# Gates of the first 1024 tokens by seven quarter products, and attention's row sums with three direct products per group

## The chip, the cores and the metric

The kernel runs on one core of a Trainium2 chip. The time is device time in microseconds (us) from the start to the end of one execution. The engines are named as the profile names them: PE does matrix products (PEld its weight loads), DVE, ACT and POOL do elementwise work, SP issues most of the DMAs; SPq, POOLq and ACTq are the DMA queues that SP, POOL and ACT feed.

## The reference, cut to what matters

One layer over 2048 latent tokens of width 1024, with 256 context tokens. Both parts that are changed stand in these lines:

```python
mod_l = (s_lat @ w_mod[l] + b_mod[l])[:, None, :]
sh1, sc1, g1, sh2, sc2, g2 = jnp.split(mod_l, 6, axis=-1)
h = _modulate(_rms(x, norm1_g[l]), sh1, sc1)
p = h @ w_in[l]                                   # 1024 -> q, kv, k_pe, f, gates
...
s = jnp.einsum('bqhd,bkhd->bhqk', q, k) * (QK_DIM ** -0.5)
pr = jax.nn.softmax(s, axis=-1)                   # 2048 queries, 2304 keys, 8 heads
o = jnp.einsum('bhqk,bkhd->bqhd', pr, v)
...
ga = jax.nn.sigmoid(p[..., OFF_GA:OFF_GB])        # 1024 columns
gb = jax.nn.sigmoid(p[..., OFF_GB:N_IN])          # 1024 columns
x = x + g1 * ((ga * (attn_o @ w_o_attn) + gb * (four_o @ w_fourier)) @ w_out)
```

A mixture of experts follows on the result; the change does not touch it.

## The kernel before, in words

**Number format.** PE multiplies in fp32r. For close to fp32 accuracy each factor is kept as a high part (a cast, ACT) and a low part (the value less its cast, DVE): `split`, L143 to L146. One product of two split factors is three PE products (`mm3`, L154 to L163: high by high on L159, high by low on L160, low by high on L161).

**Stage A, the combined projection.** The tokens are four blocks `g` of 512 (a fifth holds the context). Normalized and transposed, they stay split in SBUF as `hT[g]`, eight slices of 128 channels each. The columns of `w_in` are 25 tiles `j` of 128. `load_w` (L199 to L205) loads one tile (512 KB) into the single buffer `wraw` and splits it into `whi` and `wlo`, of which there are three each. One projection of one tile and block is 8 slices times 3 = 24 PE products of 128x512 into one PSUM bank (`proj`, L240). `finish` (L210) applies the sigmoid to a gate and stores it.

The plan (L463 to L480) goes through j = 5..8 (input of the Fourier branch, `fourier_fold`, L430, with fp32 products against `dft`), 1, 2 (part of the query projection), and 9..24 (the gates). Each j does all its blocks before the next; for j = 20..24 only g = 0..2 are done here, block 3 of these five tiles (`gates`, L538 to L544) in the next stage. The weights of the next j are loaded while one j is worked on.

**Steps woven in.** `mod_rows` (L395) forms the remaining entries of `mod_l`: 8 chunks of 512 columns, each from 8 loads of 256 KB of `w_mod` into two buffers `wmr`, one multiply-add on DVE for each into `acc`, then a PE product with a column of ones (`md<-acc,ones`, L411) that sums over the partitions, a DVE add of the bias and a store of the row. `gated_wout` (L415) then loads `w_out` in 16 pieces of 256 KB into the same two buffers, scales each by `g1` on DVE (L426) and stores it through POOL's queue (L427). Before, two such steps follow each gate projection.

**Attention.** The scores of one head and 512 queries are a `group`; there are 32 (L1047 to L1106). For each of 18 key blocks `kt`, PE makes `P` (three products, L1093 to L1095), ACT takes the exponential (L1096) and its cast `phi`, DVE the rest `plo`. PE multiplies `phi` and `plo` by the values (L1066, L1067, `pv`). The denominators need the sum of `phi` over the keys: for `kt` in `ONE` (L816) by one more PE product with the column `z1` (L1069), for the others by an add on POOL into `acc` (L149), which ends as the split `ah`, `al` in two PE products (`fin`, L1071).

**What sets the order.** A scheduler gives each engine a fixed order of its instructions before the run, from program order and its own costs; at run time each engine takes them in that order and waits by semaphores. A buffer is written again only when its last reader is done. The listings of order below are those fixed orders.

Of the kernel before, what the change touches and what calls it, by code (L numbers as in the profile page):

```python
# [12 lines left out]
F = mybir.dt.float32  # L13
R = mybir.dt.float32r
# [4 lines left out]
AF = mybir.ActivationFunctionType  # L19
OP = mybir.AluOpType  # L20
# [4 lines left out]
D = 1024  # L25
# [86 lines left out]
def layer_kernel(ctx: ExitStack, tc: tile.TileContext, a: dict, out: bass.AP, stop: str = ""):  # L112
    nc = tc.nc

    def pool(es, name, bufs=1, **kw):
        return es.enter_context(tc.tile_pool(name=name, bufs=bufs, reuse_waits="tile", **kw))
# [90 lines left out]
    def terms(w, g):  # L207
# [12 lines left out]
    def tokens(g):  # L220
        return slice(g * 512, min((g + 1) * 512, NK))
# [6 lines left out]
    def gate_dst(j, g):  # L228
        return (ga_d if j < 8 else gb_d)[j % 8, :, tokens(g)]

    with ExitStack() as es:
        hp = pool(es, "hT", side="right")
        psm = pool(es, "psMA", 4, space=PSUM)
        pst = pool(es, "psTA", 2, space=PSUM)
# [34 lines left out]
        with ExitStack() as es2, ExitStack() as es_mod, ExitStack() as es_x:  # L269
# [3 lines left out]
            mp = pool(es_mod, "modw", 2, side="right")  # L273
# [17 lines left out]
            ws = []  # L291
# [77 lines left out]
            for j, w in zip(first[:2], ws):  # L369
                proj(w, 4, dst_of(j, 4))  # L370

            raw = wp.tile([128, D], F, name="wraw", bufs=1)
# [16 lines left out]
        with ExitStack() as es2:  # L389
            mp = pool(es2, "mod", 1, side="right")  # L390
            fp = pool(es2, "fold", 1, side="right")
            dft = fp.tile([128, 129], F, name="dft")
            nc.sync.dma_start(dft, a["c_dft"])

# [70 lines left out]
            w = load_w(wp, order[0])  # L465
            for n, j in enumerate(order):
                nxt = load_w(wp, order[n + 1]) if n + 1 < len(order) else None
                if 5 <= j < 9:
                    fourier_fold(j - 5, w)
                elif j < 5:  # L470
                    for g in range(4):
                        proj(w, g, dst_of(j, g))
                else:
                    for g in range(4 if j < 20 else 3):
# [4 lines left out]
            for _ in rows:  # L479
                pass  # L480
    if stop == "A":
        es_h3.close()
        es_coef.close()
        return
# [1141 lines left out]
```

## Time and profile before

| | |
|---|---|
| median of 3 runs | 2800.54 us (2798.35 to 2807.73) |
| the profiled execution | 2791.65 us |
| its span in the trace | 2789.8 us |
| mean granted clock of PE | 0.98 |
| busy: PE, PEld, DVE, ACT, POOL | 96%, 79%, 65%, 51%, 34% |
| PE products in the trace | 14148 |

The span is the time between the first and the last instruction that the trace shows; the profiled execution is 1.85 us longer. A share of busy time is a mean over stages: PE is busy nearly everywhere, the other engines are so in some stages only. Stage A's projections run from 160 to 645 us, the gates from 320 on; attention from 930 to 1800.

### The profile page before, as it was taken

What the parts mean: (1) busy time and instruction counts of PE and PEld (TensorE: products, weight loads), DVE (VectorE), ACT (ScalarE), POOL (GpSimd) and SP (SyncE); (2) the same over time, 40 slices, a digit from 0 to 9 for tenths busy, and PEclk for the clock granted to TensorE, in tenths of its full rate; (3) what the DMA queues carried; (4) which work ended last, traced back from release to release, by engine and by line L of the source; (5) the groups of instructions that cost most, each with busy time, mean ns of one, the idle gap of its engine ahead of it and who ended that gap; (6) DMA issues with size and microseconds to landing.
All of it is one profiled execution on the core that took longest, in us unless ns stands there. A gap on an engine that the chain in (4) does not pass through costs nothing.

```text
span 2789.8 us, 39364 instructions
## 1 busy us (share of the span) xinstructions
PE 2664.5 (96%) x14148; PEld 2194.8 (79%) x14148; DVE 1824.5 (65%) x3286; ACT 1415.8 (51%) x2437; POOL 954.9 (34%) x826
## 2 busy tenths in 40 slices
PE   6999999999999999999999999999995699999997
PEld 4778777787878777777777777778884699999997
DVE  6632133205567899899999999776766666666663
ACT  6511111114666588888888888823224344444441
POOL 3000000102454477777688776710004211111110
PEclk9999999999999999999999999999997799999999
DMA  6220255524667411011011100286544577878773
GB/s 228 106 79 29 94 164 158 192 76 135 175 191 207 158 28 36 17 29 32 19 42 36 26 19 8 67 257 196 176 153 135 164 227 236 242 229 233 229 223 70
DMA packets 207164, 357.40 MB, mean 128 GB/s; under 512 B 49216, under 2 KB 116484, under 8 KB 205944
## 3 DMA queue, kind: packets, MB, share of 16 engines
q1 hardware_dynamic: 156680, 241.82, 27.7%
q0 software_dynamic: 17616, 60.31, 8.6%
q10 hardware_dynamic: 32672, 52.75, 5.4%
q8 instruction: 111, 1.82, 0.3%
q14 instruction: 85, 0.70, 0.1%
HBM read 262.23 MB, written 92.59 MB: 127 GB/s over the span
## 4 chain that ended last, share of the span: by engine, by line
PE 81%; DVE 6%; DMA 5%; ACT 3%; issue 2%; POOL 2%; SPq 0%; POOLq 0%; ACTq 0%; DVEq 0%
PE mm L159 7%; PE mm L160 6%; PE mm L161 6%; PE S L924 5%; PE P L1093 4%; PE P L1094 4%; PE Ob L1067 4%; PE Oa L1066 4%; PE P L1095 4%; PE pa L160 4%; PE pa L161 4%; PE pa L159 4%; PE p L161 3%; PE p L159 2%; PE p L160 2%
## 5 line engine op out<-in xcount | busy, mean ns | idle before, releaser
L149 POOL TENSOR_TENSOR acc<-acc,phi 128x512 f32<-128x512 f32 x384 | 495.9, 1291 | 117.5 <-ACT phi L145 100.0
L146 DVE TENSOR_TENSOR plo<-P,phi 128x512 fp32r<-128x512 f32 x576 | 384.6, 681 | 26.6 <-ACT phi L145 23.1
L925 DVE TENSOR_REDUCE mxs<-S 128x1 f32<-128x1024 f32 (+1 forms) x384 | 365.3, 951 | 46.7 <-PE S L924 44.2
L1096 ACT ACTIVATE P<-P 128x512 f32<-128x512 f32 x576 | 333.8, 586 | 90.1 <-PE P L1095 75.6
L145 ACT CAST ewhi<-ewraw 128x1024 fp32r<-128x1024 f32 x181 | 190.1, 1050 | 313.1 <-PE pa L160 192.4
L145 ACT CAST phi<-P 128x512 fp32r<-128x512 f32 x576 | 332.9, 588 | 22.4 <-POOL acc L149 0.7
L159 PE MATMUL mm<-hh,whi 128*128 128x512 f32 (+1 forms) x792 | 312.1, 396 | 0.0
L160 PE MATMUL mm<-hl,whi 128*128 128x512 f32 (+1 forms) x792 | 311.5, 394 | 0.0
L161 PE MATMUL mm<-hh,wlo 128*128 128x512 f32 (+1 forms) x792 | 310.1, 392 | 0.0
L146 DVE TENSOR_TENSOR ewlo<-ewraw,ewhi 128x1024 fp32r<-128x1024 f32 x181 | 218.6, 1221 | 127.8 <-ACT ewhi L145 127.5
L160 PE MATMUL pa<-xTl,ewhi 128*128 128x256 f32 x1024 | 290.9, 284 | 3.7 <-DVE xTl L146 3.7
L159 PE MATMUL pa<-xTh,ewhi 128*128 128x256 f32 x1024 | 291.1, 284 | 0.0
L161 PE MATMUL pa<-xTh,ewlo 128*128 128x256 f32 x1024 | 289.6, 283 | 0.0
L1093 PE MATMUL P<-qh,kh 97*128 97x512 f32 x576 | 231.1, 401 | 2.1 <-DVE qh L931 1.3
L1094 PE MATMUL P<-ql,kh 96*128 96x512 f32 x576 | 228.9, 397 | 0.0
L1095 PE MATMUL P<-qh,kl 96*128 96x512 f32 x576 | 227.7, 395 | 0.0
L1066 PE MATMUL Oa<-phi,vv 128*128 128x512 f32 x576 | 224.0, 402 | 0.2 <-ACT phi L145 0.2
L1067 PE MATMUL Ob<-plo,vv 128*66 128x512 f32 x576 | 216.2, 398 | 0.5 <-DVE t L1082 0.3
L924 PE MATMUL S<-kh,qh 96*128 96x512 f32 (+1 forms) x640 | 199.1, 376 | 5.3 <-DVE mxs L925 5.2
L160 PEld LDWEIGHTS pa<-xTl,ewhi 128*128 128x128 f32 x1024 | 193.8, 189 | 9.9 <-DVE xTl L146 6.9
L159 PEld LDWEIGHTS pa<-xTh,ewhi 128*128 128x128 f32 x1024 | 193.6, 189 | 2.2 <-ACT xTh L145 0.2
L161 PEld LDWEIGHTS pa<-xTh,ewlo 128*128 128x128 f32 x1024 | 193.6, 189 | 0.2
(497 smaller groups left out, 5605.7 us busy)
## 6 DMA issues: line engine op xcount, KB each, us to landing
ewraw<-in_w_gate_t_dram SPq DMA_DIRECT2D x64, 512.0 KB
ewraw<-in_w_up_t_dram SPq DMA_DIRECT2D x64, 512.0 KB
ewraw<-in_w_e_down_dram SPq DMA_DIRECT2D x64, 512.0 KB
wmr<-in_w_mod_dram SPq DMA_DIRECT2D x64, 256.0 KB
wraw<-in_w_in_t_dram SPq DMA_DIRECT2D x30, 512.0 KB
wm<-in_w_mod_t_dram SPq DMA_DIRECT2D x32, 256.0 KB
ga_d<-oA ACTq DMA_DIRECT2D x32, 256.0 KB
gb_d<-oA ACTq DMA_DIRECT2D x32, 256.0 KB
```

Of the source, the lines that this page charges most:

```text
L145: (nc.scalar.copy if eng == "a" else nc.vector.tensor_copy)(hi, src)
L146: nc.vector.tensor_tensor(lo, src, hi.bitcast(F), op=OP.subtract)
L149: nc.gpsimd.tensor_tensor(o, x, y, op=op)
L159: nc.tensor.matmul(ps, lh, rh, start=i == 0, stop=False)
L160: nc.tensor.matmul(ps, lh, rl, start=False, stop=False)
L161: nc.tensor.matmul(ps, ll, rh, start=False, stop=i == n - 1 and not extra)
L924: nc.tensor.matmul(S[:, d:e], q[:96, j * 128:(j + 1) * 128], k[:96, c0 + d:c0 + e], start=True, stop=True)
L925: nc.vector.tensor_reduce(mxs[:, c:c + 1], S[:, :w], axis=AX.X, op=OP.max)
L1066: nc.tensor.matmul(ps["a"], v[:, kt, 0:128], hi, start=kt == 0, stop=kt == KT - 1)
L1093: nc.tensor.matmul(S, k[:, c], qh, start=True, stop=False)
L1094: nc.tensor.matmul(S, k[:96, c], ql, start=False, stop=False)
L1095: nc.tensor.matmul(S, l[:, c], qh[:96], start=False, stop=True)
```

## The change

**Gates.** For the tokens of blocks 0 and 1 the 16 gate tiles are taken in eight pairs (j, j+1). A pair is a product of a 2x2 arrangement of token quarters (block 0 or 1, channel slices 0 to 3 or 4 to 7) with a 2x2 arrangement of weight quarters (tile j or j+1, the same slices). `wino` forms it with seven products of sums of quarters (the Winograd form of Strassen's scheme) in place of eight. One product of quarters is 4 slices times 3 = 12 PE products. Sums of tokens are formed once: `token_sums`, 16 totals of 3 DVE adds in PSUM and a split each, written over `hT[1]` and `hT[2]`, and into a new tile `s1`. Sums of weights are formed for each pair: 4 DVE subtractions and 7 splits, in a ring of six tiles. The results are put together from PSUM by one ACT copy and five DVE adds per pair, four sigmoids and four stores.

Since `hT[1]` and `hT[2]` are written over, block 2 of all 16 tiles is projected first, then block 3 of j = 9..19, with the weights loaded again for each: each j has one block of 24 products there. The token sums are formed beside these 27 projections. `wino` follows them.

**Loads.** A weight tile comes as two halves of 256 KB, each with one raw buffer of its own, two projections ahead in place of one.

**Woven steps.** Three steps of `mod_rows` and `gated_wout` now follow each of the blocks of `fourier_fold` and of j = 1, 2; two still follow each gate projection. All are done before `wino`. On PE, the eight column sums of `mod_rows` stood 96 products apart before; they stand 72, 81, 55, 57, 82, 61 and 63 products of 128x512 apart now, by the order.

**Attention.** `ONE` has three key blocks in place of four: one PE product with `z1` fewer in a group, one add on POOL more.

The diff, cut to its core:

```diff
-    def load_w(wp, j):
-        raw = wp.tile([128, D], F, name="wraw", bufs=1)
-        nc.sync.dma_start(raw, a["w_in_t"][j])
+    def load_raw(wp, j, p=""):
+        raw = [wp.tile([128, 512], F, name=f"wraw{p}{h}", bufs=1) for h in range(2)]
+        for h in range(2):
+            nc.sync.dma_start(raw[h], a["w_in_t"][j, :, h * 512:(h + 1) * 512])
+        return raw
+    def load_w(wp, j):
         hi = wp.tile([128, D], R, name="whi")
         lo = wp.tile([128, D], R, name="wlo")
-        split(hi, lo, raw, "a")
+        for d, raw in zip((slice(0, 512), slice(512, D)), load_raw(wp, j)):
+            split(hi[:, d], lo[:, d], raw, "a")
...
+        def token_sums(es):
+            (h1, l1), (h2, l2), (hS, lS) = hT[0], hT[1], hT[2]
+            p = pool(es, "s1", 1, side="right")
+            s1 = p.tile([128, 4, 512], R, name="s1h"), p.tile([128, 4, 512], R, name="s1l")
+            def total(dst, k, *xs):
+                t = pst.tile([128, 512], F, name="pt")
+                for n, (op, x) in enumerate(xs[1:]):
+                    nc.vector.tensor_tensor(t, t if n else xs[0].bitcast(F), x.bitcast(F), op=op)
+                split(dst[0], dst[1], t, "a")
...
+                    total((s1[0][:, k], s1[1][:, k]), k, a21[0], (P, a21[1]), (P, a22[0]), (P, a22[1]))
...
+                    total(a21, k, a11[0], (M, a21[0]), (M, a21[1]), (P, a11[1]))
...
+                    total(s2, k, s1[0][:, k], (M, a11[0]), (M, a11[1]), (P, s1[1][:, k]))
...
+                    total((hS[:, 4 + k], lS[:, 4 + k]), k, a12[0], (M, s2[0]), (M, s2[1]), (P, a12[1]))
...
+        def wino(up, s1):
...
+            blocks = [part(hT[0], lo4), part(hT[2], lo4), part(hT[0], hi4), part(hT[1], lo4), s1, part(hT[1], hi4), part(hT[2], hi4)]
...
+                for j in range(9, 25, 2):
+                    b11, b21 = load_raw(wp, j)
+                    b12, b22 = load_raw(up, j + 1, "b")
+                    t2 = up.tile([128, 512], F, name="t2")
+                    put(b11)
+                    sub(b11, b12, b11)
+                    yield
+                    sub(t2, b22, b11)
+                    put(t2)
...
+                    sub(b12, b22, b12)
+                    put(b12)
...
+                    sub(b21, b21, t2)
+                    put(b21)
...
+                    put(b22)
...
+                    if i == 0:
+                        v["u"] = up.tile([128, 512], F, name="u")
+                        nc.scalar.copy(v["u"], ps[0])
+                    elif i == 1:
+                        nc.vector.tensor_tensor(v["u"], ps[1], v["u"], op=OP.add)
+                    elif i == 2:
+                        out(j, 0, ps[0])
+                    elif i == 3:
+                        v["u3"] = up.tile([128, 512], F, name="u3")
+                        nc.vector.tensor_tensor(v["u3"], ps[2], v["u"], op=OP.add)
+                    elif i == 4:
+                        out(j + 1, 1, ps[3], v["u3"])
+                    elif i == 5:
+                        out(j, 1, ps[2], v["u"])
+                    else:
+                        out(j + 1, 0, ps[3], v["u"])
+                for i, b in enumerate((0, 1, 0, 2, 3, 2, 3)):
...
+                    t = ring.pop(0)
+                    for k in range(4):
+                        ah, al = blocks[i][0][:, k], blocks[i][1][:, k]
+                        for m, (l, r) in enumerate(((t[:, 0, k], ah), (t[:, 0, k], al), (t[:, 1, k], ah))):
+                            nc.tensor.matmul(ps[b], l, r, start=fresh and k + m == 0, stop=k == 3 and m == 2, skip_group_check=True)
...
@@ fourier_fold
                     nc.scalar.copy(f[:, tokens(g)], ps)
+                    for _ in range(3):
+                        next(rows, None)
...
-            order = [5, 6, 7, 8, 1, 2] + list(range(9, 25))
+            plan = [(j, range(4)) for j in (5, 6, 7, 8, 1, 2)] + [(j, (2,)) for j in range(9, 25)] + [(j, (3,)) for j in range(9, 20)]
+            ws = [load_w(wp, j) for j, gs in plan[:2]]
...
+                if n + 2 < len(plan):
+                    ws.append(load_w(wp, plan[n + 2][0]))
...
+                if n == 4:
+                    es_fold.close()
+                    S1 = token_sums(es)
+                if n == 6:
+                    sums = S1[1]
+                for g in gs:
+                    if j < 5:
                         proj(w, g, dst_of(j, g))
+                        next(rows, None)
+                    else:
                         proj(w, g, gate_dst(j - 9, g), AF.Sigmoid)
-                        next(rows, None)
-                        next(rows, None)
-                w = nxt
+                        next(sums, None)
+                    next(rows, None)
+                    next(rows, None)
...
+        with ExitStack() as es2:
+            wino(pool(es2, "wino", 1), S1[0])
...
-        ONE = (5, 9, 13, 17)
+        ONE = (6, 12, 17)
```

The first place is SP in the column sums of `mod_rows` (`wmr` from `w_mod`; `row` the bias, `row_d` the stored row; `wraw` the projection's weights). Before:

```order
L402 DMA wmr<-in_w_mod_dram 128x512 x6
L201 DMA wraw<-in_w_in_t_dram 128x1024
L413 DMA row_d<-row 1x512
L402 DMA wmr<-in_w_mod_dram 128x512 x2
L409 DMA row<-in_b_mod_dram 1x512
L402 DMA wmr<-in_w_mod_dram 128x512 x6
L201 DMA wraw<-in_w_in_t_dram 128x1024
```

After (the numbers behind `wraw` tell tiles apart):

```order
L203 DMA wraw_2316<-in_w_in_t_dram 128x512
L535 DMA wmr<-in_w_mod_dram 128x512 x6
L546 DMA row_d<-row 1x512
L535 DMA wmr<-in_w_mod_dram 128x512 x2
L542 DMA row<-in_b_mod_dram 1x512
L535 DMA wmr<-in_w_mod_dram 128x512 x5
L203 DMA wraw_2493<-in_w_in_t_dram 128x512
L535 DMA wmr<-in_w_mod_dram 128x512
L203 DMA wraw_2494<-in_w_in_t_dram 128x512
```

Between two loads of a projection's weights there stood eight loads of `w_mod`; now there stand more, and a weight's second half stands behind another one of them.

The second place is SP where the gates are projected (`w_out` pieces into the same two `wmr` buffers). Before:

```order
L201 DMA wraw<-in_w_in_t_dram 128x1024
L424 DMA wmr<-in_w_out_dram 128x512
L413 DMA row_d<-row 1x512
L424 DMA wmr<-in_w_out_dram 128x512 x6
L201 DMA wraw<-in_w_in_t_dram 128x1024
L424 DMA wmr<-in_w_out_dram 128x512 x5
L201 DMA wraw<-in_w_in_t_dram 128x1024 x6
```

After, in the first projections of block 2:

```order
L203 DMA wraw_2693<-in_w_in_t_dram 128x512
L203 DMA wraw_2694<-in_w_in_t_dram 128x512
L557 DMA wmr<-in_w_out_dram 128x512 x2
L203 DMA wraw_2735<-in_w_in_t_dram 128x512
L203 DMA wraw_2736<-in_w_in_t_dram 128x512
L557 DMA wmr<-in_w_out_dram 128x512 x2
L203 DMA wraw_2783<-in_w_in_t_dram 128x512
L203 DMA wraw_2784<-in_w_in_t_dram 128x512
L557 DMA wmr<-in_w_out_dram 128x512 x2
L203 DMA wraw_2825<-in_w_in_t_dram 128x512
L203 DMA wraw_2826<-in_w_in_t_dram 128x512
```

Each weight had six or so loads of `w_out` ahead of it while one tile did four blocks; now two loads of `w_out` stand between the weights of two tiles that do one block each.

The third place is POOL in attention (`ql` the query's low part, `vv` the values of a later head). Before, one group between its first add and the next group's:

```order
L149 TENSOR_TENSOR ql<-qraw,qh 96x512
L149 TENSOR_TENSOR acc<-phi 128x512
L149 TENSOR_TENSOR acc<-acc,phi 128x512
L877 TENSOR_TENSOR vv_7902<-vraw,vv_7902 128x6x64
L149 TENSOR_TENSOR acc<-acc,phi 128x512 x11
L149 TENSOR_TENSOR ql<-qraw,qh 96x512
L149 TENSOR_TENSOR acc<-phi 128x512
```

After:

```order
L149 TENSOR_TENSOR ql<-qraw,qh 96x512
L149 TENSOR_TENSOR acc<-phi 128x512
L149 TENSOR_TENSOR acc<-acc,phi 128x512
L1025 TENSOR_TENSOR vv_8478<-vraw,vv_8478 128x6x64
L149 TENSOR_TENSOR acc<-acc,phi 128x512 x12
L149 TENSOR_TENSOR ql<-qraw,qh 96x512
L149 TENSOR_TENSOR acc<-phi 128x512
L149 TENSOR_TENSOR acc<-acc,phi 128x512 x13
```

A group has one add more, and nothing else on POOL has moved past them.

## Rows read from the trace of the kernel before

**Rows 1.** Windows of the gates and of attention; PE's granted clock
```profile
core 0: us, PE busy (x) PEld busy (x) DVE busy (x) ACT busy (x) POOL busy (x), PEclk, DMA share, GB/s
320.00:624.00 304.00, 304.00 (x1287) 238.18 (x1287) 72.94 (x94) 44.91 (x67) 8.66 (x16) 1.00 0.45 146
930.00:1800.00 870.00, 861.14 (x3771) 652.57 (x3772) 792.13 (x1203) 725.55 (x1340) 647.18 (x522) 0.99 0.12 34
```

**Rows 2.** Chain of waits by line, 267 to 645 us
```profile
by line: PE mm L159 32.7%; PE mm L161 32.3%; PE mm L160 32.3%; PE md L411 2.0%; PE md L456 0.5%; SPq L575 0.2%; issue 0.0%
```

**Rows 3.** Timeline, ACT: start, length, instruction, idle time before it
```profile
627.48 1.05 ACT L145 CAST whi<-wraw 128x1024 fp32r<-128x1024 f32 x1 [4.77 <-PE mm L160]
...
644.28 1.05 ACT L145 CAST whi<-wraw 128x1024 fp32r<-128x1024 f32 x1 [4.77 <-PE mm L160]
```

**Rows 4.** Groups by line and form, weights' split and the fold
```profile
L146 DVE TENSOR_TENSOR wlo<-wraw,whi 128x1024 fp32r<-128x1024 f32 x2 | 2.5, 1225 | 25.1 <-ACT whi L145 25.1
...
L440 DVE TENSOR_TENSOR f<-f 128x1023 f32<-128x1023 f32 x4 | 4.9, 1225 | 0.1
...
L461 DVE COPY xc<-md 128x4 f32<-128x4 f32 x8 | 1.3, 166 | 7.9 <-ACT xc L459 7.9
```

**Rows 5.** Timeline, one column sum: PE, DVE and SP
```profile
334.23 1.02 PE L411 MATMUL md<-acc,ones 128*1 128x512 f32 x2
...
335.29 0.68 DVE L412 TENSOR_TENSOR row<-md,row 1x512 f32<-1x512 f32 x1 [4.47 <-PE md L411]
...
336.39 1.11 SPq L402 DMA_DIRECT2D wmr<-in_w_mod_dram  x2
...
339.34 0.75 DVE L406 SCALAR_TENSOR_TENSOR acc<-wmr,sl,acc 128x512 f32<-128x512 f32 x1 [2.19 <-DMA wmr<-in_w_mod_dram]
...
348.22 0.75 DVE L406 SCALAR_TENSOR_TENSOR acc<-wmr,sl,acc 128x512 f32<-128x512 f32 x1 [0.63 <-DMA wmr<-in_w_mod_dram]
```

**Rows 6.** DMA issues (KB, us to landing) and timeline, `w_out`
```profile
wog_d<-wmr POOLq DMA_DIRECT2D x16, 256.0 KB, 2.7
...
501.79 0.33 SPq L424 DMA_DIRECT2D wmr<-in_w_out_dram  x1
...
505.61 1.35 DVE L426 TENSOR_TENSOR wmr<-wmr,g1b 128x512 f32<-128x512 f32 x2 [5.51 <-DMA wmr<-in_w_out_dram]
...
532.17 0.69 DVE L426 TENSOR_TENSOR wmr<-wmr,g1b 128x512 f32<-128x512 f32 x1 [2.86 <-DMA wmr<-in_w_out_dram]
...
533.16 0.54 POOL L427 DMA_DIRECT2D wog_d<-wmr  x1 [3.01 <-DVE wmr L426]
535.73 0.69 DVE L426 TENSOR_TENSOR wmr<-wmr,g1b 128x512 f32<-128x512 f32 x1 [2.86 <-DMA wmr<-in_w_out_dram]
```

**Rows 7.** Windows, during those stores and at the next stage's start
```profile
530.00:540.00 10.00, 10.00 (x45) 8.14 (x44) 1.78 (x3) 2.14 (x3) 1.23 (x3) 1.00 0.55 185
650.00:655.00 5.00, 2.80 (x9) 1.56 (x9) 3.73 (x5) 3.52 (x5) 0.96 (x1) 0.79 0.95 334
655.00:660.00 5.00, 5.00 (x14) 3.91 (x14) 4.25 (x4) 1.50 (x3) 1.66 (x2) 0.53 0.12 44
```

**Rows 8.** Groups by line and form, attention, 930 to 1800 us
```profile
L149 POOL TENSOR_TENSOR acc<-acc,phi 128x512 f32<-128x512 f32 x379 | 489.4, 1291 | 117.2 <-ACT phi L145 100.0 <-PE P L1095 0.4 <-PE S L924 0.2
L146 DVE TENSOR_TENSOR plo<-P,phi 128x512 fp32r<-128x512 f32 x569 | 379.7, 681 | 22.9 <-ACT phi L145 19.3
L145 ACT CAST phi<-P 128x512 fp32r<-128x512 f32 x569 | 328.8, 588 | 21.9 <-POOL acc L149 0.7
...
L1069 PE MATMUL Ob<-phi,z 128*66 128x512 f32 x124 | 49.4, 398 | 0.0
...
L145 ACT CAST ah<-acc 128x512 fp32r<-128x512 f32 x31 | 19.3, 623 | 10.5 <-POOL acc L149 10.3
```

**Rows 9.** Timeline, POOL near the end of attention
```profile
1752.00 4.03 POOL L149 TENSOR_TENSOR acc<-acc,phi 128x512 f32<-128x512 f32 x3
...
1760.09 1.29 POOL L149 TENSOR_TENSOR acc<-phi 128x512 f32<-128x512 f32 x1 [4.07 <-ACT phi L145]
```

More of the change, by code (lines that the diff above doesn't have):

```diff
@@ L387, in layer_kernel, with steps @@
                 nc.scalar.dma_start(kpe_d[:, tokens(g)], o[:32, :n])
-        with ExitStack() as es2:
-            mp = pool(es2, "mod", 1, side="right")
-            fp = pool(es2, "fold", 1, side="right")
+        def token_sums(es):
[7 more added lines that the diff above has]
+                split(dst[0], dst[1], t, "a")
+            def steps():
+                P, M = OP.add, OP.subtract
+                for k in range(4):
+                    a11, a12 = (h1[:, k], l1[:, k]), (h1[:, 4 + k], l1[:, 4 + k])
+                    a21, a22 = (h2[:, k], l2[:, k]), (h2[:, 4 + k], l2[:, 4 + k])
+                    total((s1[0][:, k], s1[1][:, k]), k, a21[0], (P, a21[1]), (P, a22[0]), (P, a22[1]))
+                    yield
+                    yield
+                    total(a21, k, a11[0], (M, a21[0]), (M, a21[1]), (P, a11[1]))
+                    yield
+                    yield
+                for k in range(4):
+                    a11, a12 = (h1[:, k], l1[:, k]), (h1[:, 4 + k], l1[:, 4 + k])
+                    s2 = hS[:, k], lS[:, k]
+                    total(s2, k, s1[0][:, k], (M, a11[0]), (M, a11[1]), (P, s1[1][:, k]))
+                    yield
+                    total((hS[:, 4 + k], lS[:, 4 + k]), k, a12[0], (M, s2[0]), (M, s2[1]), (P, a12[1]))
+                    yield
+            return s1, steps()
@@ new lines, in wino, with weights, put, out @@
+        def wino(up, s1):
+            lo4, hi4 = slice(0, 4), slice(4, 8)
+            part = lambda t, k: (t[0][:, k], t[1][:, k])
+            blocks = [part(hT[0], lo4), part(hT[2], lo4), part(hT[0], hi4), part(hT[1], lo4), s1, part(hT[1], hi4), part(hT[2], hi4)]
+            ring = []
+            def weights():
+                n = 0
+                def put(x):
+                    nonlocal n
+                    t = wp.tile([128, 2, 512], R, name="wlo" if n % 2 else "whi")
+                    n += 1
+                    split(t[:, 0], t[:, 1], x, "a")
+                    ring.append(t.rearrange("p s (k c) -> p s k c", k=4))
+                sub = lambda o, x, y: nc.vector.tensor_tensor(o, x, y, op=OP.subtract)
+                for j in range(9, 25, 2):
[4 more added lines that the diff above has]
+                    sub(b11, b12, b11)
+                    yield
+                    sub(t2, b22, b11)
+                    put(t2)
+                    yield
+                    put(b21)
+                    yield
+                    sub(b12, b22, b12)
+                    put(b12)
+                    yield
+                    put(b11)
+                    yield
+                    sub(b21, b21, t2)
+                    put(b21)
+                    yield
+                    put(b22)
+                    yield
+            def out(j, g, x, y=None):
+                o = st.tile([128, 512], F, name="oA")
+                if y is not None:
+                    nc.vector.tensor_tensor(o, x, y, op=OP.add)
+                nc.scalar.activation(o, x if y is None else o, AF.Sigmoid)
+                nc.scalar.dma_start(gate_dst(j - 9, g), o)
+            ahead = weights()
+            for _ in range(5):
+                next(ahead)
+            late = None
+            for j in range(9, 25, 2):
+                ps, v = [None] * 4, {}
+                def after(i, j=j, ps=ps, v=v):
+                    if i == 0:
[15 more added lines that the diff above has]
+                for i, b in enumerate((0, 1, 0, 2, 3, 2, 3)):
+                    if ps[b] is None:
+                        ps[b] = psm.tile([128, 512], F, name="mm")
+                        fresh = True
+                    else:
+                        fresh = False
+                    t = ring.pop(0)
+                    for k in range(4):
+                        ah, al = blocks[i][0][:, k], blocks[i][1][:, k]
+                        for m, (l, r) in enumerate(((t[:, 0, k], ah), (t[:, 0, k], al), (t[:, 1, k], ah))):
+                            nc.tensor.matmul(ps[b], l, r, start=fresh and k + m == 0, stop=k == 3 and m == 2, skip_group_check=True)
+                    del t
+                    if late:
+                        late()
+                    late = lambda i=i, after=after: after(i)
+                    next(ahead, None)
+            late()
@@ L392, in layer_kernel @@
+        with ExitStack() as es2, ExitStack() as es_fold:
+            mp = pool(es2, "mod", 1)
+            fp = pool(es_fold, "fold", 1, side="right")
             dft = fp.tile([128, 129], F, name="dft")
```

17 lines of the change are left out of this document (8 added, 9 removed).

## The prediction

> **What bounds the kernel now.** I read the windows of the two stretches first, then the chain of waits, then the groups and single instructions. In both stretches PE is the bound. Between 320 and 624 us, where gates are projected, PE is busy 304.0 of 304 us at a granted clock of 1.00, with DVE at 72.9, ACT at 44.9 and the DMA engines at a share of 0.45 [rows 1]. The chain from 267 to 645 us is 97% the three lines of `mm3`, and 2.0% the column sums [rows 2]. So a product removed there is worth its full length, and a new wait costs its full length. In attention PE is busy 861 of 870 us, but DVE stands at 792, ACT at 726 and POOL at 647 [rows 1]: there a product removed is worth its length only if the other three keep up.
>
> The length of a product comes from two casts of weights, 72 products apart (three blocks of 24 for one of the last tiles) with PE never idle: 644.28 less 627.48 is 16.80 us, or 0.2333 us per 128x512 product [rows 3]. The mean of 0.39 us that a group row shows is longer because products overlap [rows 8]. A block of 24 is thus 5.6 us, a pair of gate tiles in the new scheme (7 x 12 = 84 products) 19.6 us.
>
> **Gates.** Two blocks by 16 tiles were 32 x 24 = 768 products and are now 8 x 84 = 672. 96 x 0.2333 = -22.4 us.
>
> What is added stands on other engines. A pass of DVE over 128x512 is 0.68 us and a cast on ACT 0.59 [rows 8]. The token sums are 16 x 4 passes, 43.5 us of DVE, beside 27 projections of 5.6 us. Eleven weights more are loaded and split, 11 x 1.225 = 13.5 us [rows 4]. A pair costs 16 passes of DVE = 10.9 us, and 12 of ACT = 7.1 us, beside its 19.6 us of PE; its 1 MB of weights and four stores of 256 KB are 2.1 MB by 19.6 us, 107 GB/s, against 146 carried now [rows 1]. All fits with room, and I take 0 for it; if the cover is gone, rival C prices it.
>
> **Column sums.** PE waits in order at each `md<-acc,ones`. One chunk's chain is read from a single sum: PE's product at 334.23, the row add at 335.29, loads issued at 336.39, first use at 339.34, last multiply-add ending at 348.97 [rows 5]. From row add to that end it is 13.7 us; with 0.95 for the product and 0.3 around it 14.9 us. Before, 96 products = 22.4 us lay between two sums, so nothing was late (4.47 us of idle before the row add is slack). By the order they are now 72, 81, 55, 57, 82, 61 and 63 products apart. 72, 81 and 82 (16.8 us and more) hold. The gap of 55 is 12.8 + 0.95 = 13.8 us: 1.1 late. That of 57 has a fold's fp32 products in it (about 2 us, 16.3 in all); DVE's fold there is two passes of 1.225 and four of half that, with 2.0 of waiting for ACT before the small copies (7.9 over four folds) [rows 4], some 7 us, of which I let 4.1 fall on the chain: 19.0, or 2.7 late. At 61 and 63 (15.2 and 15.6) weight halves stand between the loads of `w_mod` on SP; I estimate 17 for the chain from the 1.1 us that SP takes for two issues [rows 5], so 1.8 and 1.5 late. Together **+7**; bounds 1 (only the 55) and 12 (the fold wholly on the chain).
>
> **Weights in the first pass over block 2.** This is what I fear most. Each tile now does 24 products (5.6 us) and needs its 512 KB; between the weights of two tiles SP has two loads of `w_out`, which wait for `wmr`, that is, for a scaling of the piece before on DVE and its store through POOL. Such a turn is load + 0.69 (DVE) + 0.65 (POOL's issue) + 2.7 to 2.9 (store) [rows 6]. With the 2.95 us that an undisturbed load takes [rows 5] it is 7.0; the trace of before has one piece each 3.56 us over two buffers, 7.1 per turn, at 185 GB/s [rows 6, 7]; while a weight was also landing, a load took 3.82 [rows 6], which makes 8.2. Twelve pieces stand so among the weights of j = 12 to 19. The third weight is there 2.7 us into the stretch (an estimate, a load less its issue); after five turns and a shorter sixth the ninth weight is ready at 46.9 (load of 2.95), 50.3 (3.3) or 54.7 (3.8), and PE wants it at 8 x 5.6 = 44.8. So 2.1, 5.7 or 9.9 us are lost. I take 3.3, since the stretch asks for some 251 GB/s, above the 185 seen in it and below the 334 that the next stage's start shows [rows 7]: **+5.7**, bounds 0 and 21 (rival B).
>
> The Trainium skill's page "DMA: Bandwidth & Descriptors", section "Anatomy of one DMA — SWDGE (gpsimd) path", gives about 2.0 us fixed plus bytes by 436 GB/s, which would be an estimate of 2.6 us for 256 KB. The trace has 2.95 for a load and 2.7 for a store, so the rule is a little short; by it, with that store, the turn would be 6.6, nothing would be late here, and the sum would be 5.7 lower.
>
> **Clock.** At the next stage's start PE is busy 2.80 of 5 us and the granted clock 0.79; in the 5 us behind it is 0.53, close to the lower of the clock's two levels (1.2 of 2.4 GHz), with 14 products [rows 7] where full speed makes 21. So a stall of about 2 us can cost as much again behind it. The waits above are 1 to 3 us each and apart from each other: **+3**, bounds 0 and 10.
>
> **Stage boundary.** The next stage's first loads lie over `hT[1]`, which is free one product of quarters (2.8 us) before the end now, one block (5.6) before it then: **+0.5**, bounds 0 and 2.8.
>
> **Attention.** 32 products with `z1` go: 32 x 0.2333 = -7.5 us. 32 adds of 1.291 on POOL come [rows 8], 41 us into 223 us of idle. Near the end POOL has no idle: three adds in 4.03 us, one behind the other [rows 9], and one add more in such a group costs 1.34; two such groups make **+2.7**. ACT waits for POOL before `ah<-acc`, 10.3 us over 31 casts [rows 8]; one add more in a chain that runs late there makes **+1.0**. Both together lie between 0 and 15 (a third of the new adds uncovered).
>
> **Sum.** -22.4 + 7 + 5.7 + 3 + 0.5 - 7.5 + 2.7 + 1.0 = -10.0 us against the profiled execution's own 2791.65 (span 2789.8), so 2781.6. That execution lies 8.9 us below the median shown, 2800.54, and so does what is priced in it; the forecast for a median is 2790.5 us.
>
> **Rivals.** A, the covers hold: loads stay at 2.95 us, only the 55-product gap is late, the clock costs 1 and POOL 1.5: -22.4 + 1.1 + 2.1 + 1 + 0.5 - 7.5 + 1.5 = -23.7, a median of 2777. For it: DMA at half its share before [rows 1]. Against: the gaps by the order are shorter than the chain.
>
> B, the stream of weights decides, and the kernel is slower: a load takes 5.0 us in the first pass over block 2, since weights, `w_out`, stores and gates share the DMA engines. A turn is then 9.8 us (store included), the ninth weight is ready at 65.8, PE loses 21.0, and waits of that size cost the clock 10: -10.0 + 15.3 + 7 = +12.3, a median of 2813. It breaks even from a load of about 4.3 us. For it: 3.82 us at a lighter load, and 5.51 us of waiting before that scaling [rows 6]. Against: 334 GB/s were carried elsewhere [rows 7]. The Trainium skill's page "DMA: Bandwidth & Descriptors", section "Queues, rings and completion order", says that each DMA engine serves the queues with work in turn, packet by packet; that would lengthen a load when three queues are busy, and no row shows the turns.
>
> C, the products of quarters starve: at the third or sixth product of a pair PE needs a PSUM bank or a ring tile that DVE has not freed yet. At 1.5 us for each of eight pairs and 3 for the clock: -10.0 + 12 + 3 = +5, 2805.5. For it: DVE's results and the weights' splits are in one order, so that a split stands behind an add that waits for PE. Against: DVE is busy 10.9 of 19.6 us.
>
> **How the numbers follow.** Forecast 0.42 (its own range 2781 to 2800, from the bounds of sums, weights and clock), A 0.24, B 0.22, C 0.12. The range of 2768 to 2814 takes A and most of B in. A run of this kernel tells a change of 0.3%, 8.4 us, from none: faster is below 2792. Of the forecast 0.25 lies there, with A 0.49; within 0.3% lie 0.15 of the forecast, 0.09 of C and 0.03 of B, 0.27; the rest, 0.24, is slower.
>
> **What would show it.** In the profile of the changed kernel: 128 products of PE fewer than 14148 (96 of gates, 32 with `z1`); casts of weights 5.6 us apart in the passes over blocks 2 and 3 if the stream holds, more than that from the ninth tile on if not; idle of PE before `md<-acc,ones` with DVE's `acc` as the releaser at the gaps of 55, 57, 61 and 63; pairs of 19.6 us, with DVE under 60% busy; a clock under 1.00 only behind those idle times; in attention 853 or so us of PE and more POOL, with the wait before `ah` at 11 to 12 us. The prediction is wrong if pairs take over 20.5 us, if loads of 256 KB take under 3 or over 4 us in the first pass, or if attention gets longer.

## The result and the profile after

The changed kernel is faster, and by more than the range allowed: its median is 2765.78 us (2760.45 to 2767.88, 4 runs) against 2799.44 for the kernel before (4 runs), ratio 0.988 with an interval of 0.9858 to 0.9902. The forecast was 2790.5, the range 2768 to 2814. A second comparison gave 2770.88 against 2796.02, ratio 0.9896 (0.9881 to 0.9912). So the gain is 25 to 34 us by the medians; the miss of the range's lower end is 2 us in the first comparison, and the second median lies inside it, but the middle of the forecast is 20 to 25 us too slow in both.

The profiled execution of the changed kernel took 2765.04 us, its span is 2763.2. The marks on PE below are read from the timelines of two profiles of each kernel (the second ones are e1 and e4 below), in us:

| stretch | before | before, again | changed | changed, again |
|---|---|---|---|---|
| start to the end of the last gate product | 649.9 | 649.9 | 632.2 | 631.0 |
| idle from there to the next stage's first product | 1.2 | 2.1 | 4.5 | 5.8 |
| next stage, to attention's first `P` | 284.2 | 283.6 | 279.9 | 286.5 |
| attention, to its last `Ob` | 876.5 | 877.3 | 868.7 | 867.8 |
| from there to the last expert product | 963.3 | 961.4 | 963.5 | 967.0 |

The mean of the two pairs is -18.3 in the first row, +3.5 in the second, -8.7 in the fourth. The third and fifth rows, which the change doesn't touch, differ by 7 and 4 us between two executions of one and the same changed kernel: nothing is read from them.

The second row is a longer wait, but not all of it is lost. In the kernel before, other waits of the next stage follow. In the 40 us from the last gate product PE idles 5.4 us before (7.7 in the second profile) and 6.0 in the changed kernel (7.1), by these windows, first before, then changed:

```profile
649.93:689.93 40.00, 34.64 (x138) 27.71 (x138) 28.75 (x77) 17.73 (x31) 10.94 (x12) 0.83 0.44 137
632.19:672.19 40.00, 33.96 (x153) 28.22 (x152) 30.97 (x87) 21.48 (x39) 11.51 (x13) 0.91 0.49 150
```

The windows of the gates, in the three parts that the changed kernel has (first pass over block 2 with `w_out`; the rest of the passes; the eight pairs), answer to [rows 1]:

```profile
core 0: us, PE busy (x) PEld busy (x) DVE busy (x) ACT busy (x) POOL busy (x), PEclk, DMA share, GB/s
318.00:375.00 57.00, 57.00 (x246) 45.73 (x246) 25.65 (x40) 15.70 (x27) 7.59 (x14) 1.00 0.72 236
375.00:470.00 95.00, 95.00 (x416) 77.72 (x415) 46.05 (x71) 36.42 (x66) 0.00 (x0) 1.00 0.49 158
470.00:632.00 162.00, 162.00 (x696) 129.79 (x694) 84.96 (x128) 58.97 (x99) 0.00 (x0) 1.00 0.37 114
```

PE is never idle in any of the three, and the clock stays at 1.00. Where I forecast 5.7 us of waiting for weights there is none, at 236 GB/s. The trace has 14020 products of PE, 128 fewer, as forecast. The pairs take 19.6 us each (first product at 469.77, last one ending at 626.73, by 8), with DVE at 52%: rival C did not happen.

PE's waits at the column sums, by its timeline (the idle time before an instruction and what ended it stand in brackets), answer to [rows 5]:

```profile
235.45 1.02 PE L544 MATMUL md<-acc,ones 128*1 128x512 f32 x2 [0.51 <-DVE acc L539]
...
294.11 0.59 PE L544 MATMUL md<-acc,ones 128*1 128x512 f32 x1 [0.72 <-DVE acc L539]
...
311.68 1.02 PE L544 MATMUL md<-acc,ones 128*1 128x512 f32 x2 [1.65 <-DVE acc L539]
```

That is 2.9 us in three places, not 7. By the order the places are the gaps of 55, 61 and 63 products, forecast at 1.1, 1.8 and 1.5 us and measured at 0.5, 0.7 and 1.65. At the gap of 57, with the fold in it, I forecast the longest wait (2.7), and there is none, in either profile of the changed kernel. DVE's last multiply-add and PE's sum there:

```profile
252.01 0.75 DVE L539 SCALAR_TENSOR_TENSOR acc<-wmr,sl,acc 128x512 f32<-128x512 f32 x1 [0.94 <-DMA wmr<-in_w_mod_dram]
...
253.84 1.02 PE L544 MATMUL md<-acc,ones 128*1 128x512 f32 x2
```

The chain is 1.1 us early. It took 16.25 us from row add to last multiply-add where I had 17.75, and PE needed 18.4 us from sum to sum where I had 16.3.

### The profile page after: what moved, and what is told of

It is laid out like the page before. It is cut to its first block, busy times and chain, and to the rows that moved or that the text cites. A ratio compares the mean times of both kernels' runs of the same rounds, so it can differ in the third digit from the quotient of the medians.

```text
span 2763.2 us, 39800 instructions
## 1 busy us (share of the span) xinstructions
PE 2629.2 (95%) x14020; PEld 2175.5 (79%) x14020; DVE 1955.7 (71%) x3530; ACT 1461.0 (53%) x2569; POOL 1000.7 (36%) x858
## 4 chain that ended last, share of the span: by engine, by line
PE 51%; DVE 5%; DMA 3%; issue 2%; POOL 2%; ACT 1%; SPq 0%; ACTq 0%; POOLq 0%; DVEq 0%
PE pa L160 4%; PE pa L161 4%; PE pa L159 4%; PE S L1072 4%; PE P L1241 4%; PE P L1242 4%; PE P L1243 4%; PE Oa L1214 4%; PE Ob L1215 4%; PE p L161 3%; PE p L160 2%; PE p L159 2%; PE py L1711 2%; PE py L1713 2%; PE py L1712 2%
## 5 line engine op out<-in xcount | busy, mean ns | idle before, releaser
L149 POOL TENSOR_TENSOR acc<-acc,phi 128x512 f32<-128x512 f32 x416 | 538.0, 1293 | 48.3 <-ACT phi L145 23.1
L1214 PE MATMUL Oa<-phi,vv 128*128 128x512 f32 x576 | 214.8, 397 | 1.7 <-ACT phi L145 1.5
L159 PE MATMUL mm<-hh,whi 128*128 128x512 f32 (+1 forms) x536 | 211.0, 396 | 1.1 <-DVE oA L221 1.1
L160 PE MATMUL mm<-hl,whi 128*128 128x512 f32 (+1 forms) x536 | 210.5, 394 | 0.0
L161 PE MATMUL mm<-hh,wlo 128*128 128x512 f32 (+1 forms) x536 | 209.4, 391 | 0.0
```

The source lines that it names most:

```text
L149: nc.gpsimd.tensor_tensor(o, x, y, op=op)
L159: nc.tensor.matmul(ps, lh, rh, start=i == 0, stop=False)
L160: nc.tensor.matmul(ps, lh, rl, start=False, stop=False)
L161: nc.tensor.matmul(ps, ll, rh, start=False, stop=i == n - 1 and not extra)
```

## What the experiments showed

### e1 to e4: the kernels again, and each part alone

e1 and e4 are the two kernels unchanged. e2 is the kernel before with attention's edit alone, e3 the changed kernel with that edit undone:

```diff
-        ONE = (5, 9, 13, 17)      # e2, on the kernel before
+        ONE = (6, 12, 17)
-        ONE = (6, 12, 17)         # e3, on the changed kernel
+        ONE = (5, 9, 13, 17)
```

> The kernel before, unchanged, timed and profiled once more. My forecast carried the 8.9 us between the first profiled execution (2791.65) and the median (2800.54) over to the changed kernel. If that gap belongs to the kernel (a profiled execution is always shorter), the new profile is again some 9 us below the median. If it was one execution that happened to be quick, the new profile lies anywhere from 2792 to 2808 and the difference sits in the stage after the gates, from 650 to 935 us, where the granted clock fell to 0.5 behind short idle times; the gates and attention are then as long as in the first profile to within 1 us (494.2 and 876.5 us).

> The kernel before with only attention's direct sums changed, three key blocks in place of four. Theory (the cover holds): attention from the first P to the last Ob is 32 x 0.2333 = 7.5 us shorter, 876.5 to 869, and nothing else moves: ratio 0.9973. The prediction's value with POOL late in two groups: 3.8 us shorter, 872.7, ratio 0.9986.

> The changed kernel with attention's four direct sums put back. Theory: from the end of the context block to the first product of the next stage 478 us as in the changed kernel (494 before), so 16 us less, and some 4 less in the next stage if its idle times fall as in the changed kernel; attention 876.5 us as before. Sum -18 to -20, ratio 0.993. If the two parts are not additive (attention shorter because it starts after another history of the clock), attention here is shorter than 874.

> The changed kernel, unchanged, timed beside the three others and profiled once more. Theory: -26.6 us by the two profiles is the real size and the rest of the 33.7 between the medians is spread of executions: ratio 0.9885 to 0.9905, and the stage after the gates again 280 us (279.9) if its gain of 4.3 us belongs to the change, or up to 285 if it was an accident of the clock.

Measured, against the kernel before: e1 0.9994 (0.9982 to 1.0005), e2 0.9965 (0.9951 to 0.9979), e3 0.9944 (0.9927 to 0.9961), e4 0.9896 (0.9881 to 0.9912). By these ratios, of the 2796 us beside them: -10 for attention's edit, -16 for the gates, -29 for both (-10, -17 and -25 by the medians); the parts add up within their intervals.

e1's profiled execution is quick again (2790.71 us, 2.9 below the median of its 12 runs), but e4's is 3.8 above its median, with a span of 2772.9 where the first one had 2763.2. So the 8.9 us that I carried over from the first profile are not a constant of profiling: two executions of the changed kernel differ by 10 us. The lines here are the whole next stage, first of the changed kernel, then of the same kernel again; the granted clock goes with the length:

```profile
637.00:916.00 279.00, 260.40 (x1456) 226.10 (x1455) 191.00 (x564) 161.39 (x337) 121.21 (x158) 0.98 0.63 189
```

```profile
637.00:923.00 286.00, 264.04 (x1456) 230.22 (x1456) 196.56 (x567) 161.57 (x337) 119.38 (x158) 0.96 0.62 184
```

The -4.3 of the first pair of profiles in that stage was an accident. Attention is not one: 876.5 (e3), 877.3 (e1) and 876.5 with four direct sums; 867.4 (e2), 867.8 (e4) and 868.7 with three.

### e7: weights as whole tiles

```diff
-        for d, raw in zip((slice(0, 512), slice(512, D)), load_raw(wp, j)):
-            split(hi[:, d], lo[:, d], raw, "a")
+        raw = wp.tile([128, D], F, name="wraw", bufs=1)
+        nc.sync.dma_start(raw, a["w_in_t"][j])
+        split(hi, lo, raw, "a")
...
-                    b11, b21 = load_raw(wp, j)
+                    raw = wp.tile([128, D], F, name="wraw", bufs=1)
+                    nc.sync.dma_start(raw, a["w_in_t"][j])
+                    b11, b21 = raw[:, :512], raw[:, 512:]
```

> The changed kernel with each gate weight loaded and split as one tile of 512 KB in place of two halves of 256 KB; the order of loads stays. Theory (the halves hide what I forecast as late, since the second half is wanted 2.8 us after the first): without them PE idles 2 to 10 us in the first pass over block 2, where the changed kernel idles none. Rival (loads simply were quicker than I took them, 2.9 us and not 3.3): under 2 us.

PE's timeline in the first pass of e7:

```profile
355.50 0.50 PE L161 MATMUL mm<-hh,wlo 128*128 128x512 f32 x1 [1.49 <-DVE wlo L146]
...
361.35 0.50 PE L159 MATMUL mm<-hh,whi 128*128 128x512 f32 x1 [0.46 <-ACT whi L145]
...
364.05 0.50 PE L161 MATMUL mm<-hh,wlo 128*128 128x512 f32 x1 [1.96 <-DVE wlo L146]
...
370.03 0.50 PE L159 MATMUL mm<-hh,whi 128*128 128x512 f32 x1 [0.59 <-ACT whi L145]
...
372.12 0.50 PE L161 MATMUL mm<-hh,wlo 128*128 128x512 f32 x1 [1.35 <-DVE wlo L146]
```

These are 5.85 us, where my term was 5.7, and with the waits behind them the idle time of the first pass lies within the 2 to 10 us of the theory. But the cause is not the one that I had priced. Around the ninth tile (SP and DVE):

```profile
364.02 0.33 SPq L210 DMA_DIRECT2D wraw<-in_w_in_t_dram  x1
...
370.85 1.22 DVE L146 TENSOR_TENSOR wlo<-wraw,whi 128x1024 fp32r<-128x1024 f32 x1
...
372.09 0.33 SPq L210 DMA_DIRECT2D wraw<-in_w_in_t_dram  x1
```

In e7 a weight is issued when the split of the tile before has released the one raw buffer. That holds for all seven weights from 322.43 to 372.09, each issued 0.03 us after a split ends. So a turn there is load, cast and split one behind the other, 8.3 us. The pieces of `w_out` lengthen its parts, but no weight waits on SP for a piece, which is what my term prices; that the loss comes near the term is luck. The same chain costs idle time later, with no `w_out` in the stream: a turn is 6.3 us there, and PE idles 8.7 us between 390 and 490, mostly half a microsecond for each projection. The next stage begins 24 us later than in the changed kernel (660.6 against 636.7). The one run took 2785.51 us. So two halves with a buffer each are needed; what of that is the finer load and what the finer release, e7 does not tell.

What the changed kernel does at the tile that I named, the ninth, stands around 360 us (SP, ACT and DVE). Its first product is at 365.1:

```profile
356.54 0.98 SPq L203 DMA_DIRECT2D wraw<-in_w_in_t_dram  x2
...
360.08 0.62 ACT L145 CAST whi<-wraw 128x512 fp32r<-128x512 f32 x1 [4.33 <-DMA wraw<-in_w_in_t_dram]
...
362.41 0.62 ACT L145 CAST whi<-wraw 128x512 fp32r<-128x512 f32 x1 [1.21 <-DMA wraw<-in_w_in_t_dram]
...
363.16 0.69 DVE L559 TENSOR_TENSOR wmr<-wmr,g1b 128x512 f32<-128x512 f32 x1 [3.05 <-DMA wmr<-in_w_out_dram]
363.77 1.28 DVE L146 TENSOR_TENSOR wlo<-wraw,whi 128x512 fp32r<-128x512 f32 x2
```

Both halves are split at 365.05, 44.7 us into the stretch that begins with the first gate product (320.31). I had forecast 50.3, and PE comes at 44.8: even as one tile it would be just in time. The next tile lives on its halves: its first product is at 370.7, and its second half is split at 373.30, which PE wants 2.8 us behind the first:

```profile
372.62 0.68 DVE L146 TENSOR_TENSOR wlo<-wraw,whi 128x512 fp32r<-128x512 f32 x1
```

The turn of the `w_out` buffers is not shorter than I took it. One of them (SP, DVE, POOL):

```profile
349.06 0.33 SPq L557 DMA_DIRECT2D wmr<-in_w_out_dram  x1
...
352.77 0.69 DVE L559 TENSOR_TENSOR wmr<-wmr,g1b 128x512 f32<-128x512 f32 x1 [2.63 <-DMA wmr<-in_w_out_dram]
...
353.76 0.54 POOL L560 DMA_DIRECT2D wog_d<-wmr  x1 [5.10 <-DVE wmr L559]
...
356.12 0.33 SPq L557 DMA_DIRECT2D wmr<-in_w_out_dram  x1
```

This one is 7.1 us; over six turns of this buffer (316.66 to 363.77) the mean is 7.85, where I chose 7.5. From issue to first use the 13 pieces for which DVE waited took 3.15 to 4.79 us, median 3.76, where I chose 3.3, and a store 3.1 (median). So the rival of e7, that loads are simply quicker, fails by the loads themselves. The gain lies in the order: between the third tile, split 2.1 us into the stretch, and the issue of the ninth (356.54) stand nine pieces, four and a half turns, because SP issues a weight between the two pieces of a pair, and not only behind the second. I had counted five turns and a sixth. The issue is thus at 36.2 us, where 2.7 and five turns of 7.5 make 40.2.

### e9: twice the pieces

```diff
+                    for again in range(2):
+                        raw = mp.tile([128, 512], F, name="wmr", bufs=2)
+                        nc.sync.dma_start(raw, a["w_out"][0, k // 2 * 128:(k // 2 + 1) * 128, d])
...
+                        nc.vector.tensor_tensor(raw, raw, g[:, d], op=OP.mult)
+                        nc.gpsimd.dma_start(wog_d[k // 2 * 128:(k // 2 + 1) * 128, d], raw)
```

> The changed kernel with each piece of w_out loaded, scaled and stored twice (the same values), so that pieces stand two by two between the weights of some 15 tiles in place of 7. Theory (a turn is 6.9 us against 5.6, the tiles start 9 us ahead and the halves give 2.8 more): 15 turns lose 20 us, less 12 of lead: PE idles about 8 us in the first pass, and the clock may fall behind it. Rival (the stream has no fixed turn; the DMA engines just carried 236 GB/s and have room): under 2 us.

PE idles 10.1 us in eight places between 370 and 440, the three longest being:

```profile
371.81 0.50 PE L159 MATMUL mm<-hh,whi 128*128 128x512 f32 x1 [1.66 <-ACT whi L145]
...
408.36 0.79 PE L161 MATMUL mm<-hh,wlo 128*128 128x512 f32 x1 [3.63 <-DVE wlo L146]
...
435.78 0.50 PE L161 MATMUL mm<-hh,wlo 128*128 128x512 f32 x1 [1.59 <-DVE wlo L146]
```

The stretch is 15.8 us longer than the changed kernel's (370.3 against 354.5 from the last fold to the last gate product): 10.1 idle, and at a clock of 0.95 over 65 us some 3.3 more, by this window of e9; the other 2.4 are not accounted for:

```profile
375.00:440.00 65.00, 56.58 (x226) 42.91 (x224) 27.29 (x43) 16.30 (x29) 8.82 (x17) 0.95 0.75 247
```

So rival B's mechanism exists, as does the clock's price behind it. In the changed kernel the pieces end as the lead does: that nothing at all is lost there is a near thing, and in part luck.

### e5: two woven steps in place of three

```diff
-                    for _ in range(3):
+                    for _ in range(2):
                         next(rows, None)
```

> The changed kernel with two woven steps after each block of the Fourier projections in place of three, so that column sums stand farther apart on PE and more of the w_out pieces come among the gate weights. Theory for the sums (a sum is late because 55 to 63 products are shorter than its chain of loads): PE's idle time at the column sums falls from 2.9 us to under 0.5. Theory for the weight stream (a turn with two pieces takes 6.9 us against 5.6 of PE, and the tiles live on the 9 us by which they are ahead): about ten such turns eat some 12 us, so PE idles 0 to 3 us there. Sum: the stretch up to the last gate product 0 to 3 us shorter than the changed kernel's. If the idle at the sums came from DVE's fold rather than from the spacing, it stays near 2.9.

The sums among the folds, now 96 products apart, no longer wait; two later ones do (0.95 and 1.01), at gaps of 60 and 62 that the edit left as short as they were. So 2.0 us are left of 2.9, where I expected under 0.5. The `w_out` pieces that now come later cost 1.9 (at 394 and 396 us). The stretch from the first fold to the last gate product is 2.9 us longer (448.9 against 446.1), not shorter; the ratio to the kernel before, 0.9909 (0.9879 to 0.994), can't be told from the changed kernel's. In both kernels every wait at a sum stands at a gap of 63 products or fewer, and a gap of 72 or more has none, as the forecast has it. Of the 4 us by which its term was too big, 2.7 are the fold's gap.

### e6 and e10: the boundary to the next stage

The next stage's first products wait for `ckvh`, the split of its input. Timelines of the changed kernel, SP, DVE and PE:

```profile
626.53 0.38 SPq L723 DMA_DIRECT2D w_kv_upg<-in_kv_a_norm_g_dram  x1
...
632.96 0.59 SPq L766 DMA_DIRECT2D ckv<-ckv_d  x1
...
631.81 1.42 DVE L729 TENSOR_SCALAR kv<-kv,w_kv_upg 128x1024 f32<-128x1024 f32 x2 [2.96 <-DMA w_kv_upg<-in_kv_a_norm_g_dram]
...
636.71 0.79 PE L159 MATMUL pu<-w_kv_uph,ckvh 128*128 128x512 f32 x1 [4.52 <-ACT ckvh L145]
```

and of the kernel before, SP and PE:

```profile
644.27 0.38 SPq L575 DMA_DIRECT2D w_kv_upg<-in_kv_a_norm_g_dram  x1
...
646.50 0.59 SPq L618 DMA_DIRECT2D ckv<-ckv_d  x1
...
651.16 0.50 PE L159 MATMUL pu<-w_kv_uph,ckvh 128*128 128x512 f32 x1 [1.22 <-ACT ckvh L145]
```

In both, SP goes on some 5.7 us before PE's last gate product ends (632.2 and 649.9). But then SP needs 6.4 us to reach `ckv` in the changed kernel, and needed 2.2: the loads of two rows of gains (`sq`), which SP had issued well ahead in the kernel before, now stand in between, and a gain column waits 1.5 us for the store of a gate. e6 moves the inputs' loads ahead of them; e10 also loads the gain column early:

```diff
 # e6
+        ahead = front(0)
         wq = load_up("w_q_up", "q_a_norm_g", 3, 768)
         grow = bp.tile([128, NH, 96], F, name="sq")
...
-        ahead = front(0)
 # e10, besides
-            gc = up.tile([128, kt], F, name=name + "g")
-            nc.sync.dma_start(gc, a[g][0].rearrange("(k p) -> p k", p=128))
+            gc = gains[name]
```

> The changed kernel with the first loads of the next stage's inputs (ckv, kpe, cq) put ahead of the loads of small constants and of the query weights on SP. Theory for the boundary (the small constants stand ahead of ckv on SP and cost some 5 us after the buffer comes free): PE's idle time between its last gate product and its first product of the next stage falls from 4.5 to 5.8 us to about 1.5, and that is the gain, 3 to 4 us. Rival (the wait is for the buffer and the landing, whatever stands ahead): it stays above 3.5.

> The changed kernel with the first inputs' loads ahead on SP, and besides the two gain columns loaded early, into a tile of their own. With the inputs alone moved, PE still idled 3.2 us at the boundary, and there the gain column was issued at 627.51 and its first use began at 633.00. Theory (the gain column, released with the last product of quarters and some 5 us on its way, is the last to come): now the idle time falls to 0 to 1 us, 4 to 5 us less than in the changed kernel. Rival (the cast of the weights or the input itself is as late): 2 to 3 us stay.

The idle time is 3.23 us in e6 and 1.33 in e10, so both loads were on the path. But e10's PE timeline shows where it went:

```profile
633.27 0.50 PE L159 MATMUL pu<-w_kv_uph,ckvh 128*128 128x512 f32 x1 [1.33 <-ACT ckvh L145]
...
636.93 0.58 PE L768 MATMUL ss<-ones,ckv 128*128 128x1 f32 x2 [2.92 <-POOL ckv L759]
```

A new wait of 2.92 us stands two products later. Together it is 4.25 against 4.52: the stage's other inputs come no sooner. e6 took 2770.13 us, ratio 0.992 (0.9891 to 0.9949); e10 2762.48, the lowest median of all, but its ratio of 0.9887 (0.9865 to 0.991) can't be told from the changed kernel's.

### e11 and e12: how far POOL's cover goes

```diff
-        ONE = (6, 12, 17)
+        ONE = (9, 17)       # e11
+        ONE = (17,)         # e12
```

> The changed kernel with two direct sums per group in attention (key blocks 9 and 17) and one more add on POOL. Four to three gave 8 to 10 us (876.9 to 868.0 in the mean of the profiles). Theory (PE is the bound of attention still and POOL's 41 us more lie in its idle time): another 7.5 to 9 us, attention 859 to 861. Rival (POOL's cover ends): attention 865 or more, with ACT's wait for POOL before its cast of acc above 25 us where the changed kernel has 15.6.

> The same with one direct sum per group (key block 17): 64 adds on POOL more than the changed kernel, 83 us. Theory of the cover: 853 us. POOL's sums, 16 adds of 1.29 us beside 27 us a group, and its other work (688 of 861 us busy now, about 770 then), say that near the end of attention, where POOL is never idle, several us come back: 855 to 862, and with the rival above 868 or more.

Attention takes 874.4 us in e11 and 923.6 in e12, where three direct sums take 867.4 to 868.7 (e2, e4 and the changed kernel). The ratios are 0.9921 (0.99 to 0.9941) and 1.0091 (1.007 to 1.0113). Groups by line in attention's stretch, of the changed kernel:

```profile
L149 POOL TENSOR_TENSOR acc<-acc,phi 128x512 f32<-128x512 f32 x416 | 538.0, 1293 | 48.3 <-ACT phi L145 23.1 <-POOL acc L149 0.3
...
L145 ACT CAST ah<-acc 128x512 fp32r<-128x512 f32 x32 | 19.9, 622 | 18.5 <-POOL acc L149 18.4
```

of e11:

```profile
L145 ACT CAST ah<-acc 128x512 fp32r<-128x512 f32 x32 | 19.9, 621 | 36.1 <-POOL acc L149 36.1
```

and of e12:

```profile
L145 ACT CAST ah<-acc 128x512 fp32r<-128x512 f32 x32 | 19.8, 619 | 85.6 <-POOL acc L149 85.6
...
L1223 PE MATMUL Ob<-ah,z 128*66 128x512 f32 x32 | 14.9, 464 | 36.0 <-ACT ah L145 36.0
```

ACT's wait for POOL's sum grows with each product taken away: 11.2 us with four (10.3 for the 31 casts of [rows 8]), then 18.4, 36.1 and 85.6 (the 15.6 that the expectation of e11 names leaves out the last of the 32 casts). It reaches PE before `Ob<-ah,z` as 0.4, 1.2 and 36.0 us. With three, POOL's adds are all but covered; with two they already cost more than the products give.

In e11 PE idles 11.6 us in attention, where the changed kernel has 4.3. Most of the difference comes by DVE, which takes its instructions in order: it sits at `al<-acc,ah`, whose `ah` waits for POOL, and PE's next operand stands behind that. The longest case (POOL, ACT, DVE, PE):

```profile
1762.94 4.01 POOL L149 TENSOR_TENSOR acc<-acc,phi 128x512 f32<-128x512 f32 x3
...
1766.99 0.62 ACT L145 CAST ah<-acc 128x512 fp32r<-128x512 f32 x1 [0.28 <-POOL acc L149]
1767.64 1.10 DVE L146 TENSOR_TENSOR al<-acc,ah 128x512 fp32r<-128x512 f32 x1 [3.88 <-ACT ah L145]
1768.74 0.69 DVE L146 TENSOR_TENSOR plo<-P,phi 128x512 fp32r<-128x512 f32 x1
1769.49 0.80 PE L1241 MATMUL P<-qh,kh 97*128 97x512 f32 x1 [3.08 <-DVE plo L146]
```

Four shorter ones (0.6 to 1.0 us of PE each, behind 1.2 to 1.6 of DVE at `al`) and the 1.2 before `Ob<-ah,z` make 7.5 us. The places of the direct sums among the key blocks change with their number in all these runs; what the places alone are worth was not tried.

## Why the prediction was wrong, point by point

- **Gates.** From the context's last transpose to the last gate product it is 513.4 us before and 494.0 after: -19.4, with 2.9 of waits in it, so -22.3 for the products against -22.4 forecast. Right.
- **Column sums, +7.** 2.9 in the first profile, 2.5 in the second. That a gap shorter than its chain waits was right, and three of the four places (55, 61, 63). The fourth and largest was wrong: the fold's gap, 2.7, measured 0. I had its chain 1.5 us too long and PE's work in that gap 2 us too short.
- **Weights, +5.7.** This is the step that failed most. I had the ninth weight ready at 50.3 (load of 3.3) when PE wants it at 44.8; it was ready at 44.7. Not the turn was too long (7.5, measured 7.85), but the number of turns ahead of that weight: nine pieces, four and a half turns, where I counted five and a sixth. The sum is also wrong in itself: 2.7 and six turns of 7.5 are 47.7, and with a turn of 7.0 they are 44.7, not 46.9. And I took the tile as one, although the order of SP that I showed has it in halves; the next tile needs that.
- **Clock, +3.** With no stretch of waits the clock of the projections and pairs stayed at 1.00: this term hung on the two above it, and failed with them. Where waits do come the price is real (e9: 15.8 us lost with 10.1 idle).
- **Boundary, +0.5.** The first wait grew by 3.5, above the bound of 2.8: I looked at when the buffer comes free, which is the same 5.7 us ahead in both, and not at what SP has to issue between that and `ckv`. But over 40 us the idle time is the same within its spread (5.4 and 7.7 before, 6.0 and 7.1 changed), so what it costs in the end is not shown to be more than the 0.5.
- **Attention, -3.8.** -8.8 (mean of the profiles with each number). I charged POOL with 3.7, and its cover held, just (e11, e12), although ACT's wait before `ah` rose to 18.4 and not to 11 to 12. A product taken away was also worth 0.27 us and not 0.2333; why is not shown.
- **The sum.** With the measured terms it is -22.4 + 2.9 + 0 + 0 - 8.8 = -28.3, or -24.8 with all of the 3.5 at the boundary; the medians gave 25 and 34. Five charges (sums, weights, clock, POOL's two) came out below what I took, together by 16.5 us. No one of them explains the miss: without the weights' term the forecast would still have been 2784.8.
- **The reference.** The 8.9 us between profile and median were added to both kernels. The changed kernel's profile lies 0.7 below its median, and later medians of the kernel before were 2792.1 to 2796.0. Without that step the forecast would have been 2781.6, still too slow.
- Rival C is refuted. Rival A's sum (-23.7, a median of 2777) is nearest, but not its reason: it has loads at 2.95 us, and they took 3.76.

## What to carry to other kernels

When several covers are each likely to hold, price each at its likeliest value, not near its upper bound: five small charges made a clear gain look like a coin toss. Count a load in the pieces in which it is issued, count what stands ahead of each piece in the issuing engine's order, and ask when each is wanted. At a stage's boundary read that whole list too, and add up the waits over the next tens of microseconds, not the first one alone. Work given to a spare engine is free until its last item stands before a consumer, or before another engine that holds the consumer's operand behind it, and then the price is steep: four, three, two and one direct sums took 877, 868, 874 and 924 us of attention.

## What the runs showed of the hardware

Two executions of the changed kernel took 279.9 and 286.5 us in a stage with many short idle times of PE, with a granted clock of 0.98 and 0.96 over that stage. An idle time of 3.6 us in e9 stood at the start of a fall of the clock (0.82 granted from 400 to 410 us); the waits of up to 1.7 us at the column sums of the changed kernel stood in windows at 1.00. But in the kernel before, waits of 1.2, 0.3 and 0.7 us stood ahead of 0.79 and 0.53 [rows 7], so the length of the single wait does not sort these cases.

With `w_out`, its stores, the weights and the gates on the DMA queues at once (236 GB/s), a load of 256 KB took 3.15 to 4.79 us from issue to first use, median 3.76, against 2.95 undisturbed [rows 5], and a store 3.1 against 2.7 [rows 6].

A gain column of 128 x 2 single values, issued at 626.53, was first used at 631.81, with DVE idle for 2.96 us until it landed: some 5 us, longer than any of those loads of 256 KB.
